# Where the 31-tap convolution of a token mixer starts on VectorE: behind the context's projections instead of behind the filler queue

## The chip, the cores and the metric

The kernel runs on one core of a Trainium2 chip. The metric is the device time of one execution in microseconds. Three executions took 2501.44, 2507.44 and 2507.93 us, median 2507.44. About 0.3% (7.5 us) is what a measurement of this kernel can tell from no change.

## What is computed

The reference is a network of two blocks on 512 tokens of width 1024: 256 tokens of context and 256 latents. The second block has two layers, and each runs four token mixers side by side and multiplies their joined results by `w_out`. In layer 0 both halves go through the mixers; in layer 1 only the latents do, with the context's keys and values.

```
def conformer_conv(a_val, a_gate, conv_w, conv_b, ln_g, ln_b):
    glu = a_val * jax.nn.sigmoid(a_gate)
    y = depthwise_conv(glu, conv_w) + conv_b
    return jax.nn.silu(layer_norm(y, ln_g, ln_b))

def token_mixers(z, k1, k2, v, rope, lam, lam_init, conv_a_w, conv_a_b, ln_a_g, ln_a_b, subln_g,
                 sg_ln_g, sg_ln_b, sg_w, sg_b, conv_d_w, w_out):
    a_val, a_gate, q, _, _, u, sv, bg, cg, xin = z
    y_a = conformer_conv(a_val, a_gate, conv_a_w, conv_a_b, ln_a_g, ln_a_b)
    q1, q2 = qk_heads(q, rope)
    y_b = diff_attention(q1, q2, k1, k2, v, lam, lam_init, subln_g)
    y_c = spatial_gating(u, sv, sg_ln_g, sg_ln_b, sg_w, sg_b)
    y_d = short_conv_mixer(bg, cg, xin, conv_d_w)
    return jnp.concatenate([y_a, y_b, y_c, y_d], axis=-1) @ w_out
```

`z` are the columns of the normalized tokens times one wide matrix. `diff_attention` is softmax attention with two score maps per head, whose weights are subtracted.

## The kernel before, in words

Every fp32 product is three fp32r matmuls (high part by high part, high by low, low by high), L287, L288 and L289 in `mm3`. A weight is loaded by a transfer on SP's queue into a `raw` tile, ScalarE casts the high part (L281, `wh`), and VectorE subtracts it for the low part (L282, `wl`). Results are split for the next product in the same way (L266 on ScalarE, L267 on VectorE).

PSUM has three pools of 512-column tiles: `pm` (4 tiles) for projections and transposes, `px` (3) for scores and small sums, `pa` (1) for the attention's result. In SBUF the tiles named `a` come from one pool of 31 buffers; casts of weights go through three `wh` and three `wl` buffers.

The change is in `_mixers`, which runs once per layer (`l` is 0 or 1). Its parts are closures and generators:

- `gated(f)` makes one half (128 of 256 channels) of the convolution's input: two projections (L1440 and L1441), a zero fill on POOL (L1442), a sigmoid on ScalarE (L1444) and a product on VectorE (L1446), which goes into a padded tile and is appended to `glu`.
- `taps()` is the 31-tap convolution, all of it on VectorE: for each `f` one TENSOR_SCALAR (L1488) and 30 SCALAR_TENSOR_TENSOR (L1490) that add into the tile `ya_f`. It yields every two taps, 15 times per half.
- `qk_of` and `v_of` project queries, keys and values.
- `gating()` is the spatial gating (GELU at L1548 and L1549, its layer norm at L1550 to L1560, product with a second matrix, L1571), `short()` the short convolution, and `conv_norm()` (L1717 to L1736) the layer norm and SiLU (L1733) behind the taps.
- `probs` is one attention item, 128 queries of one head: scores on TensorE (L1647, two `px` tiles), maximum (L1650, L1651), exponential on ScalarE (L1654), reciprocal and factors (L1657, L1658), scaling (L1659, L1660). `mix` transposes its weights (L1238) and multiplies them with the values into `pa`; it runs two items later.
- `fill()` is a queue of filler work for TensorE: in layer 0 the latents' queries, keys and values; then `gated(0)` and `gated(1)`; then the steps of `gating` and `short`; and last the projections by `w_oa`.

The loop at the end runs over the items, 16 in layer 0 (8 of the context with 256 keys, 8 of the latents with 512) and 8 in layer 1. Each turn issues an item's `probs`, one or two steps of the filler, and, once both halves of `glu` exist, some steps of the taps. So the text sets an order of priority; a scheduler then places the instructions of the five engines, and each engine executes its own in that fixed order. An instruction that waits holds up all that stand behind it on the same engine.

Of the kernel before, what the change touches and what calls it, by code (L numbers as in the profile page):

```python
# [1194 lines left out]
def _rotate(K, x, kind, tab):  # L1195

    nc = K.nc
    ps = K.ax_ps()
    nc.tensor.matmul(ps[:, 0:TC], K.perm[kind], x, start=True, stop=True)
    t = K.t2()  # L1200
    nc.vector.tensor_mul(t[:, 0:TC], ps[:, 0:TC], tab[:, 1])
    nc.vector.tensor_mul(x, x, tab[:, 0])
    nc.vector.tensor_add(x, x, t[:, 0:TC])
# [205 lines left out]
def _mixers(K, l, h, z, mod, norm):  # L1409
# [24 lines left out]
    glu = []  # L1434

    def gated(f):

        pv_, pg = K.mm_ps(), K.mm_ps()
        K.proj(W(6 + f), 1, lambda k: h[k], pg[:, a:e], a, e)
        K.proj(W(4 + f), 1, lambda k: h[k], pv_[:, a:e], a, e)  # L1440
        t = K.a4(F32, (P, seqs, TC + 30))  # L1441
        nc.gpsimd.memset(t, 0.0)  # L1442
        s = K.t2()
        nc.scalar.activation(s[:, a:e], pg[:, a:e], AF.Sigmoid)  # L1444
        r = lambda x: x[:, a:e].rearrange("p (s t) -> p s t", s=seqs)
        nc.vector.tensor_mul(t[:, :, 15:15 + TC], r(s), r(pv_))  # L1446
        glu.append(t)

    def qk_of(t, ws, x0, x1):
        ps = K.mm_ps()  # L1450
        K.proj_w([ws], lambda k: h[k], ps[:, x0:x1], x0, x1)
        x = K.t2()
        nc.scalar.copy(x[:, x0:x1], ps[:, x0:x1])
        if x1 == T:
            _rotate(K, x[:, TC:T], 1, tab)
        K.split(t[:, 0, x0:x1], t[:, 1, x0:x1], x[:, x0:x1])
# [3 lines left out]
    def v_of(wv, hv):  # L1460

        vps = K.mm_ps()
        for t in range(2):
            sl = slice(hv[1] + t * P, hv[1] + (t + 1) * P)
            vv = vps[:, t * 256:(t + 1) * 256]
            for kt in range(KD):
                wh, wl = wv[kt // 4]
                K.mm3(vv, h[kt][:, 0, sl], h[kt][:, 1, sl], wh[:, kt % 4, :], wl[:, kt % 4, :],
                      kt == 0, kt == KD - 1)
            v = K.a4(F32R, (P, 2, 4, P))  # L1470
            nc.gpsimd.memset(v.bitcast(F32), 0.0)
            src = vv.rearrange("p (j e d) -> p j e d", j=2, e=2)
            dst = v.rearrange("p x (j e) c -> p x j e c", j=2)
            for g in range(2):
                K.split(dst[:, 0, :, g, 64 * g:64 * g + 64], dst[:, 1, :, g, 64 * g:64 * g + 64], src[:, :, g])
            vz.append(v)
# [4 lines left out]
    def taps():  # L1481
        for f in range(2):
            if f == 0:
                ya_f.append(K.a4())
            y3 = ya_f[0][:, f, a:e].rearrange("p (s t) -> p s t", s=seqs)
            w = lambda i: K.pvc("conv_a_w", (l * 31 + i) * 2 + f)
            x = lambda i: glu[f][:, :, i:i + TC]
            nc.vector.tensor_scalar(y3, x(0), w(0), K.pvc("conv_a_b", l * 2 + f), op0=ALU.mult, op1=ALU.add)  # L1488
            for i in range(1, 31):
                nc.vector.scalar_tensor_tensor(y3, x(i), w(i), y3, op0=ALU.mult, op1=ALU.add)  # L1490
                if i % 2 == 0:
                    yield

    conv = taps()

    def step(gen, n):
        for _ in range(n):
            next(gen, None)
# [12 lines left out]
            qk_of(qp[f], wq[f], 0, TC)  # L1511
    wv = vw(l == 1)
    v_of(wv, HALVES[0])
    if l == 1:
        for f in range(2):
            qk_of(kp[f], wk[f], TC, T)
        for f in range(2):
            qk_of(qp[f], K.weight(W(f)(0)), TC, T)
        v_of(wv, HALVES[1])


    yc = []
# [82 lines left out]
    def fill():  # L1605
        if l == 0:
            for f in range(2):
                qk_of(kp[f], wk[f], TC, T)
                yield
            for f in range(2):  # L1610
                qk_of(qp[f], wq[f], TC, T)
                yield
            v_of(vw(), HALVES[1])
            yield
        for f in range(2):
            gated(f)
            yield
        parts = {"g": gating(), "s": short()}
        for c in "ss" + "g" * nt + "sssgsg":
            next(parts[c])  # L1620
            yield
        y = yc + yd
        for ft in range(KD):
            ps = K.mm_ps()
            K.proj(lambda c: A["w_oa"][l, ft, 0], 1, lambda k: y[k], ps[:, a:e], a, e)
            K.resid(ps, z[ft // 2][:, ft % 2], mod[:, 2], ft, halves)
            yield

    filler = fill()

    yb = []
# [120 lines left out]
    for i, u in enumerate(items):  # L1752
        queue.append((u, probs(*u)))
        step(filler, FS[l][i])
        if len(glu) == 2 and conv is not None:
            step(conv, (3,2)[l])
            if next(conv, 0) == 0:
                conv = None
                tails.append(conv_norm())
        tails = [g_ for g_ in tails if next(g_, 0) is None]  # L1760
        finish(2)
# [141 lines left out]
```

## Time and profile before

| | |
|---|---|
| median of three runs | 2507.44 us |
| the profiled execution | 2502.68 us, of which its span is 2500.9 us |
| TensorE (PE) busy | 2398.7 us, 96% of the span |
| VectorE (DVE) busy | 1618.3 us, 65% |
| ScalarE (ACT) busy | 1106.4 us, 44% |
| mean granted TensorE clock | 0.978 of full speed |
| chain of work that ended last | PE 85%, DVE 6%, DMA 5%, ACT 3% |

Layer 0's mixers take the stretch from about 1552 to 1742 us, layer 1's that from about 2157 to 2300 us. A table by stretch gives, for each engine, its busy time and (in brackets) its number of instructions, then the mean granted clock of TensorE: 1.00 is 2.4 GHz, and a stretch spent at 1.2 GHz counts half. In lists of lines, a mean duration includes the fill of the engine's pipeline, which overlaps the next instruction; the step from one start to the next is a little shorter.

### The profile page before, as it was taken

The numbers are of one execution on the slowest core, as the hardware profiler recorded it, in microseconds if no ns is written. First come the engines' busy times: TensorE is split into PE (matmuls) and PEld (weight loads), VectorE is DVE, ScalarE is ACT, GpSimd is POOL, SyncE is SP. The second block draws the span as 40 slices with busy tenths as digits, with TensorE's granted clock in tenths as the row PEclk, the third lists the DMA queues.
The fourth block names the chain that finished last, engine by engine and source line by source line (L and its number), as shares of the span: only waits on it lengthen the run. The fifth ranks groups of instructions, "written<-read, shape, count | busy, mean of one in ns | idle before, by whom it ended". The sixth has DMA issues, their size and how long they took to land.

```text
span 2500.9 us, 36344 instructions
## 1 busy us (share of the span) xinstructions
PE 2398.7 (96%) x14234; PEld 2066.7 (83%) x14234; DVE 1618.3 (65%) x2953; ACT 1106.4 (44%) x1875; POOL 11.3 (0%) x20
## 2 busy tenths in 40 slices
PE   7999999999998999999999999989999999988998
PEld 4877888788897887778887999867978778977998
DVE  4856445544667675666766676897848564597665
ACT  5643334322544333235546455554523323465543
POOL 0000000000000000000000000000000000000000
PEclk9999999999999999999998999989999999998999
DMA  8565223333323455565347554222336563123553
GB/s 314 192 215 185 85 85 110 127 101 112 110 88 130 150 173 167 200 229 195 117 132 256 181 176 138 79 77 81 124 104 216 171 227 117 64 94 102 187 183 120
DMA packets 113741, 369.71 MB, mean 148 GB/s; under 512 B 12576, under 2 KB 15008, under 8 KB 113568
## 3 DMA queue, kind: packets, MB, share of 16 engines
q1 hardware_dynamic: 113568, 367.38, 44.5%
q8 instruction: 112, 1.84, 0.3%
q14 instruction: 61, 0.50, 0.1%
HBM read 357.89 MB, written 9.44 MB: 147 GB/s over the span
## 4 chain that ended last, share of the span: by engine, by line
PE 85%; DVE 6%; DMA 5%; ACT 3%; issue 1%; SPq 0%; DVEq 0%; ACTq 0%
PE pm L287 23%; PE pm L288 23%; PE pm L289 22%; PE px L287 4%; PE px L289 4%; PE px L288 4%; DMA raw<-in_ada 2%; DVE wl L282 1%; PE pa L423 1%; PE px L313 1%; DVE a L465 1%; PE px L1647 1%; DMA raw<-in_w_inb 1%; DVE a L1490 1%; PE pm L1238 1%
## 5 line engine op out<-in xcount | busy, mean ns | idle before, releaser
L287 PE MATMUL pm<-a,wh 128*128 128x512 f32 (+1 forms) x2432 | 838.3, 346 | 7.4 <-DVE a L267 4.2
L289 PE MATMUL pm<-a,wl 128*128 128x512 f32 (+1 forms) x2432 | 834.0, 344 | 3.6 <-DVE wl L282 3.6
L288 PE MATMUL pm<-a,wh 128*128 128x512 f32 (+1 forms) x2432 | 835.9, 344 | 0.0
L281 ACT CAST wh<-raw 128x1024 fp32r<-128x1024 f32 (+2 forms) x421 | 420.2, 1002 | 810.4 <-PE pm L288 454.2
L282 DVE TENSOR_TENSOR wl<-raw,wh 128x1024 fp32r<-128x1024 f32 (+2 forms) x421 | 487.8, 1161 | 330.3 <-ACT wh L281 326.6
L287 PEld LDWEIGHTS pm<-a,wh 128*128 128x128 f32 x2432 | 462.6, 191 | 78.7 <-ACT wh L281 10.7
L289 PEld LDWEIGHTS pm<-a,wl 128*128 128x128 f32 x2432 | 463.2, 191 | 58.0 <-DVE wl L282 4.6
L288 PEld LDWEIGHTS pm<-a,wh 128*128 128x128 f32 x2432 | 464.1, 191 | 51.7 <-issue 1.0
L287 PE MATMUL pm<-a,a 128*128 128x256 f32 (+2 forms) x844 | 249.8, 302 | 14.8 <-DVE t L368 6.4
L288 PE MATMUL pm<-a,a 128*128 128x256 f32 (+2 forms) x844 | 250.3, 298 | 2.3 <-DVE a L267 1.4
L289 PE MATMUL pm<-a,a 128*128 128x256 f32 (+2 forms) x844 | 247.6, 296 | 0.0
L465 DVE SCALAR_TENSOR_TENSOR a<-raw,cs,a 128x1024 f32<-128x1024 f32 x168 | 211.2, 1279 | 54.0 <-DMA raw<-in_ada 49.8
L287 PEld LDWEIGHTS pm<-a,a 128*128 128x128 f32 x844 | 164.8, 198 | 26.4 <-issue 11.1
L288 PEld LDWEIGHTS pm<-a,a 128*128 128x128 f32 x844 | 166.8, 198 | 6.5 <-DVE a L267 3.2
L289 PEld LDWEIGHTS pm<-a,a 128*128 128x128 f32 x844 | 166.0, 197 | 2.4 <-issue 0.4
L549 DVE SCALAR_TENSOR_TENSOR a<-pm,mod,a 128x256 f32<-128x256 f32 x188 | 87.2, 479 | 82.0 <-PE pm L289 81.0
L287 PE MATMUL pm<-wh,a 128*128 128x512 f32 (+1 forms) x336 | 128.6, 385 | 3.3 <-ACT a L266 3.3
L288 PE MATMUL pm<-wl,a 128*128 128x512 f32 (+1 forms) x336 | 129.9, 387 | 0.0
L289 PE MATMUL pm<-wh,a 128*128 128x512 f32 (+1 forms) x336 | 126.1, 383 | 0.0
L266 ACT CAST a<-t 128x256 fp32r<-128x256 f32 (+2 forms) x173 | 86.0, 503 | 86.2 <-DVE t L1787 37.8
L287 PE MATMUL px<-a,wh 128*128 128x256 f32 (+1 forms) x364 | 120.3, 332 | 0.0
L289 PE MATMUL px<-a,wl 128*128 128x256 f32 (+1 forms) x364 | 119.9, 330 | 0.0
(309 smaller groups left out, 2915.7 us busy)
## 6 DMA issues: line engine op xcount, KB each, us to landing
raw<-in_ada SPq DMA_DIRECT2D x176, 512.0 KB, 4.5
raw<-in_w_m SPq DMA_DIRECT2D x128, 512.0 KB, 4.3
raw<-in_ffn_in SPq DMA_DIRECT2D x88, 512.0 KB, 4.4
raw<-in_w_qk SPq DMA_DIRECT2D x32, 512.0 KB, 3.5
raw<-in_w_v SPq DMA_DIRECT2D x32, 512.0 KB, 3.6
raw<-in_ffn_oa SPq DMA_DIRECT2D x32, 512.0 KB, 3.6
raw<-in_w_inb SPq DMA_DIRECT2D x28, 512.0 KB, 3.6
a<-in_ada SPq DMA_DIRECT2D x16, 512.0 KB, 9.0
```

The costliest lines, as they stand in the source:

```text
L266: self.nc.scalar.copy(hi, src)
L281: nc.scalar.copy(hi, raw)
L282: nc.vector.tensor_sub(lo, raw, hi.bitcast(F32))
L287: mm(out, ah, bh, start=start, stop=False)
L288: mm(out, ah, bl, start=False, stop=False)
L289: mm(out, al, bh, start=False, stop=stop)
L313: self.nc.tensor.matmul(out_ps[:, i * nt + t:i * nt + t + 1], a[:, c0 + t * P:c0 + (t + 1) * P], self.ones[:, 0:1], start=(k == 0), stop=( ...
L423: nc.tensor.matmul(ps[32 * j:32 * j + 32, 0:256], self.cs[:, l // 2, kt, :], raw[:, j, :], start=(kt == 0), stop=(kt == KD - 1), tile_posi ...
L465: nc.vector.scalar_tensor_tensor(s, raw, c, s, op0=ALU.mult, op1=ALU.add)
L549: self.nc.vector.scalar_tensor_tensor(z[:, a:b], ps[:, a:b], gate[:, kt, w:w + 1], z[:, a:b], op0=ALU.mult, op1=ALU.add)
L1238: nc.tensor.transpose(pt[:, s * P:(s + 1) * P], p[:, s * P:(s + 1) * P], K.ident)
L1490: nc.vector.scalar_tensor_tensor(y3, x(i), w(i), y3, op0=ALU.mult, op1=ALU.add)
```

## The change

`gated(0)` and `gated(1)` leave the filler queue and run right behind the context's values, before the first item. The taps get two steps there, and in layer 1 two more behind each of the latents' four query and key projections and behind their values (twelve in all ahead of the loop). In the loop they are stepped in every turn, one step (layer 0) or two (layer 1) and the one of the test for the end, two and three in all, where it was four and three from the turn on in which both halves of `glu` existed. Nothing is computed otherwise.

```
     v_of(wv, HALVES[0])
+    for f in range(2):
+        gated(f)
+    step(conv, 2)
     if l == 1:
         for f in range(2):
             qk_of(kp[f], wk[f], TC, T)
+            step(conv, 2)
         for f in range(2):
             qk_of(qp[f], K.weight(W(f)(0)), TC, T)
+            step(conv, 2)
         v_of(wv, HALVES[1])
+        step(conv, 2)
...
-        for f in range(2):
-            gated(f)
-            yield
         parts = {"g": gating(), "s": short()}
...
         step(filler, FS[l][i])
-        if len(glu) == 2 and conv is not None:
-            step(conv, (3,2)[l])
+        if conv is not None:
+            step(conv, (1, 2)[l])
             if next(conv, 0) == 0:
```

Line numbers of the changed kernel are 6 higher between the first and the last piece, and 3 higher behind it: L1650 there is L1647 here, L1653 is L1650, L1657 is L1654, L1660 is L1657 and L1663 is L1660.

**VectorE, layer 0, the start of the taps.** `a_14451` (before) and `a_14061` (changed) are the accumulators, `sd` an item's statistics, `t` its weights. Before:

```order
L1446 TENSOR_TENSOR a_14346<-t_14348,pm_14284 128x2x256
L1660 SCALAR_TENSOR_TENSOR t_14276<-t_14278,sd_14264,t_14276 128x256
L1488 TENSOR_SCALAR a_14451<-a_14346,pv 128x512
L1490 SCALAR_TENSOR_TENSOR a_14451<-a_14346,pv,a_14451 128x512 x2
L1650 TENSOR_REDUCE sd_14364<-px_14366 128x1
```

Changed:

```order
L1446 TENSOR_TENSOR a_13989<-t_13991,pm_13927 128x2x256
L282 TENSOR_TENSOR wl_14344<-raw_14341,wh_14343 128x1024
L1488 TENSOR_SCALAR a_14061<-a_13989,pv 128x512
L1490 SCALAR_TENSOR_TENSOR a_14061<-a_13989,pv,a_14061 128x512 x4
L282 TENSOR_TENSOR wl_14350<-raw_14347,wh_14349 128x1024
L1490 SCALAR_TENSOR_TENSOR a_14061<-a_13989,pv,a_14061 128x512
L1660 RECIPROCAL sd_14067<-sd_14067 128x2
L1490 SCALAR_TENSOR_TENSOR a_14061<-a_13989,pv,a_14061 128x512
L1661 TENSOR_TENSOR sd_14067<-sd_14067,lt_13697 128x2
L1490 SCALAR_TENSOR_TENSOR a_14061<-a_13989,pv,a_14061 128x512
L1663 SCALAR_TENSOR_TENSOR t_14079<-t_14081,sd_14067,t_14079 128x256
```

The first tap stood behind the sixth item's softmax (row 1684 of the engine's order); it now stands at row 1624, between the first item's maximum and its reciprocal, and all 60 taps stand ahead of the GELU's statistics, up to row 1758.

**VectorE, layer 1, the end of the taps.** Before, the last taps stand behind the eighth and last item's L1660 and behind the layer norm of the gating:

```order
L1560 TENSOR_TENSOR a_19862<-a_19862,a_19854 128x256
L1660 SCALAR_TENSOR_TENSOR t_20198<-t_20200,sd_20186,t_20198 128x512
L1560 TENSOR_TENSOR a_19862<-a_19862,a_19854 128x256
L1490 SCALAR_TENSOR_TENSOR a_19676<-a_19671,pv,a_19676 128x256
L267 TENSOR_TENSOR a_20144<-a_19862,a_20143 128x4x64
L267 TENSOR_TENSOR a_20178<-pm_20179,a_20177 128x4x128
L1490 SCALAR_TENSOR_TENSOR a_19676<-a_19671,pv,a_19676 128x256
```

Changed:

```order
L1660 RECIPROCAL sd_19869<-sd_19869 128x2
L1490 SCALAR_TENSOR_TENSOR a_19423<-a_19418,pv,a_19423 128x256
L1661 TENSOR_TENSOR sd_19869<-sd_19869,lt_19129 128x2
L1490 SCALAR_TENSOR_TENSOR a_19423<-a_19418,pv,a_19423 128x256
L1605 TENSOR_TENSOR t_19714<-t_19714,pm_19970 128x256
L1663 SCALAR_TENSOR_TENSOR t_19881<-t_19883,sd_19869,t_19881 128x512
L1653 TENSOR_REDUCE sd_19950<-px_19952 128x1
L1653 TENSOR_REDUCE sd_20054<-px_20055 128x1
```

The last tap moved from row 2544, behind every item's softmax, to row 2482, ahead of the fourth item's L1660 (L1663 in the changed file) and of the gating's layer norm.

**TensorE, layer 0, behind `conv_norm`.** `px_15189` and `px_15195`, or `px_15333` and `px_15339`, are the broadcast statistics of the convolution's norm; the L1647 (L1650) rows are scores. Before, the scores of the last two items stand there, and other products behind them:

```order
L337 MATMUL px_15189<-first,rs_15181 128x128 x4
L337 MATMUL px_15195<-first,st_15176 128x128 x4
L1647 MATMUL px_15221<-a_13711,a_13713 128x512 x3
L1647 MATMUL px_15222<-a_13711,a_13713 128x512 x3
L1696 MATMUL px_15288<-ind,a_14362 128x2 x2
L1647 MATMUL px_15312<-a_13711,a_13713 128x512 x3
```

Changed:

```order
L337 MATMUL px_15333<-first,rs_15325 128x128 x4
L337 MATMUL px_15339<-first,st_15320 128x128 x4
L1650 MATMUL px_15355<-a_13711,a_13713 128x512 x3
L289 MATMUL pm_15455<-a_14906,wl_15459 128x512
L287 MATMUL pm_15455<-a_15183,wh_15458 128x512
L288 MATMUL pm_15455<-a_15183,wh_15458 128x512
L289 MATMUL pm_15455<-a_15183,wl_15459 128x512
L1650 MATMUL px_15356<-a_13711,a_13713 128x512 x3
L1710 MATMUL px_15416<-first,sq_15417 128x128 x2
L1238 MATMUL pm_15485<-first,t_15366 128x128 x4
```

One item is left behind the norm instead of two, and its transposes (L1238 of `t_15366`) follow its own scores after four product matmuls.

## Rows read from the trace of the kernel before

**Rows 1.** The page: busy time by engine, and the chain that ended last.
```profile
PE 2398.7 (96%) x14234; PEld 2066.7 (83%) x14234; DVE 1618.3 (65%) x2953; ACT 1106.4 (44%) x1875; POOL 11.3 (0%) x20
PE 85%; DVE 6%; DMA 5%; ACT 3%; issue 1%; SPq 0%; DVEq 0%; ACTq 0%
```

**Rows 2.** Busy time by stretch, layer 0: PE, PEld, DVE, ACT, POOL, clock, DMA, GB/s.
```profile
1620.00:1640.00 20.00, 19.33 (x90) 14.88 (x88) 19.30 (x31) 10.60 (x19) 0.00 (x0) 1.00 0.50 170
1640.00:1660.00 20.00, 15.38 (x49) 11.55 (x50) 17.51 (x38) 13.25 (x25) 0.00 (x0) 0.74 0.18 54
1680.00:1700.00 20.00, 16.07 (x86) 13.12 (x86) 18.37 (x40) 10.61 (x25) 0.00 (x0) 0.83 0.05 14
1700.00:1720.00 20.00, 16.33 (x66) 12.23 (x66) 16.06 (x53) 11.79 (x23) 0.00 (x0) 0.74 0.06 15
```

**Rows 3.** The same table, layer 1.
```profile
2220.00:2240.00 20.00, 18.37 (x123) 15.27 (x122) 19.27 (x47) 11.61 (x24) 0.00 (x0) 1.00 0.23 66
2240.00:2260.00 20.00, 8.59 (x47) 6.89 (x45) 20.00 (x69) 9.82 (x22) 0.00 (x0) 0.66 0.10 27
2260.00:2280.00 20.00, 20.00 (x143) 19.65 (x144) 14.50 (x42) 9.98 (x20) 0.00 (x0) 0.83 0.18 54
```

**Rows 4.** Waits of PE in layer 1, and in layer 0: total, times, longest.
```profile
PE px L1707 <- DVE sd L1658: 7.6, 1, 7.6
PE px L313 <- DVE a L1490: 0.6, 1, 0.6
PE px L1647 <- ACT t L1654: 7.3, 3, 4.5
```

**Rows 5.** Busy time ahead of the taps and among them, both layers (columns as above).
```profile
1570.00:1598.00 28.00, 27.91 (x168) 22.90 (x166) 18.17 (x50) 16.33 (x41) 0.00 (x0) 1.00 0.20 67
1598.00:1640.00 42.00, 41.33 (x197) 32.88 (x195) 40.79 (x78) 23.08 (x39) 0.00 (x0) 1.00 0.36 119
2165.00:2193.00 28.00, 28.00 (x215) 25.87 (x213) 14.90 (x34) 11.90 (x26) 0.00 (x0) 1.00 0.19 58
2193.00:2225.00 32.00, 32.00 (x201) 27.21 (x200) 30.57 (x66) 21.32 (x35) 0.00 (x0) 1.00 0.37 123
```

**Rows 6.** DVE by line and shape, layer 0 (1552 to 1742), then layer 1.
```profile
L1490 DVE SCALAR_TENSOR_TENSOR a<-a,pv,a 128x512 f32<-128x512 f32 x60 | 44.1, 739 | 0.1
L1490 DVE SCALAR_TENSOR_TENSOR a<-a,pv,a 128x256 f32<-128x256 f32 x60 | 27.2, 472 | 0.1
```

**Rows 7.** DVE in order of time: start, us, what.
```profile
1666.38 0.67 DVE L1650 TENSOR_REDUCE sd<-px 128x1 f32<-128x512 f32 x1
1666.98 0.73 DVE L1490 SCALAR_TENSOR_TENSOR a<-a,pv,a 128x512 f32<-128x512 f32 x1
1667.64 0.15 DVE L326 SCALAR_TENSOR_TENSOR rs<-rs 128x4 f32<-128x4 f32 x1
...
1668.38 1.21 DVE L282 TENSOR_TENSOR wl<-raw,wh 128x1024 fp32r<-128x1024 f32 x1
1669.52 0.74 DVE L1490 SCALAR_TENSOR_TENSOR a<-a,pv,a 128x512 f32<-128x512 f32 x1
```

**Rows 8.** DVE in order of time, layer 1: five taps in a row, and the last.
```profile
2235.54 2.05 DVE L1490 SCALAR_TENSOR_TENSOR a<-a,pv,a 128x256 f32<-128x256 f32 x5
2237.52 0.15 DVE L1657 RECIPROCAL sd<-sd 128x2 f32<-128x2 f32 x1
...
2259.32 0.47 DVE L1490 SCALAR_TENSOR_TENSOR a<-a,pv,a 128x256 f32<-128x256 f32 x1
```

**Rows 9.** PE in order of time at full clock: 512 columns, 256 columns, scores.
```profile
1613.59 0.40 PE L287 MATMUL pm<-a,wh 128*128 128x512 f32 x1
1613.83 0.39 PE L288 MATMUL pm<-a,wh 128*128 128x512 f32 x1
...
1566.25 0.62 PE L1647 MATMUL px<-a,a 32*128 32x256 f32 x6
1566.81 0.44 PE L1238 MATMUL pm<-first,t 128*128 128x128 f32 x2
...
1567.20 0.28 PE L288 MATMUL pm<-a,a 128*128 128x256 f32 x1
1567.32 0.29 PE L289 MATMUL pm<-a,a 128*128 128x256 f32 x1
```

**Rows 10.** ACT in order of time: behind the convolution's norm in layer 0.
```profile
1708.68 0.62 ACT L266 CAST a<-a 128x512 fp32r<-128x512 f32 x1
1709.20 0.58 ACT L266 CAST a<-pm 128x512 fp32r<-128x512 f32 x1
1709.80 1.28 ACT L1654 ACT_TABLE_LOAD   x1
1711.09 0.69 ACT L1654 ACTIVATE t<-px,sd 128x512 f32<-128x512 f32 x1
```

**Rows 11.** POOL's zero fills in layer 0, and transfers from 1552 to 1612.
```profile
L1442 POOL MEMSET a<- 128x572 f32 x2 | 1.1, 576 | 28.8 <-PE pm L288 28.8
...
raw<-in_w_inb SPq DMA_DIRECT2D x2, 512.0 KB, 3.2
```

## Prediction

> **What bounds the kernel now.** I read the page's busy table first. TensorE is busy for 96% of the span and makes 85% of the chain that ended last [rows 1], so time can come back only where TensorE stands idle or runs at 1.2 GHz. Next I read the tables by stretch around the two mixers, and took as lost, in each 20 us, what is missing from busy time times granted clock. In layer 0 that is 20 - 19.33 = 0.7, 20 - 15.38 x 0.74 = 8.6, 20 - 16.07 x 0.83 = 6.7 and 20 - 16.33 x 0.74 = 7.9, together 23.9 us [rows 2]. In layer 1 it is 20 - 18.37 = 1.6, 20 - 8.59 x 0.66 = 14.3 and 20 - 20 x 0.83 = 3.4, together 19.3 us [rows 3]. In these stretches VectorE is busy for 80% to 100%, and the waits of TensorE name it or an exponential that hangs on it; the largest in layer 1 is one of 7.6 us [rows 4]. Ahead of the taps VectorE has time left: 28 - 18.2 = 9.8 us from 1570 to 1598 and 28 - 14.9 = 13.1 us from 2165 to 2193, and among the taps almost none (40.79 of 42, 30.57 of 32) [rows 5]. So **the taps stand where VectorE is short, behind a stretch in which it is idle**. No more than 23.9 + 19.3 = 43 us can come back.
>
> **Unit prices.** A tap's mean is 739 ns on 512 columns and 472 on 256 [rows 6], with an overlapped part; from start to start a tap takes 1667.64 - 1666.98 = 0.66, a maximum over 512 columns 0.60, the low part of a 1024-column weight 1669.52 - 1668.38 = 1.14, the smallest instruction 0.07 to 0.08 [rows 7]. Five taps on 256 columns take 1.98 us, 0.396 each [rows 8]. TensorE takes 0.24 per product of 512 columns, 0.12 per product of 256, and 0.093 per score product on 256 keys [rows 9]. The sums below are instruction counts of the changed order times these steps.
>
> **Layer 0, ahead of the norm.** TensorE's first product with new values behind the gating's first stretch waits for VectorE's L267 at row 1763. From the first L1446 to that row VectorE has 146 instructions: 60 taps x 0.66 = 39.6, 10 weight parts x 1.14 = 11.4, 12 maxima of 256 at an estimated 0.34 (half of 0.60, and a little) and 2 of 512 = 5.3, and 62 others at some 0.27 on average, estimated from their sizes = 16.7; together 73 us. TensorE's work over the same part is 144 x 0.24 + 160 x 0.12 + 42 x 0.093 + some 2 for transposes = 60 us. Both begin at about the same time, VectorE some 1.6 us later because L1446 waits for the sigmoid. TensorE therefore waits 73 + 1.6 - 60 = 14.6, say **15 us**. The bounds are 11 (some of the 62 priced too high) and 18 (VectorE idles 3% of this part, as it did among the taps). It isn't returned later: behind the taps VectorE has less to do than TensorE. In exchange the losses of 0.7, 8.6 and 6.7 us of 1620 to 1700 go, since the 60 taps that kept VectorE at 97% there stand earlier. Of the first two, part is ScalarE's: GELU and exponential take turns there. That order stays, but three loads of tables fall away, because both sigmoids now stand together. Each took 1.28 us, and the exponential began 1711.09 - 1709.80 = 1.29 behind its start [rows 10], so ScalarE gets 3.9 us. I keep 2 us of loss here, between 0 (the room hides the rest) and 4 (nothing is gained). The Trainium skill, page "ScalarE: Activation LUTs", section "What ACT_TABLE_LOAD costs", puts a switch at about 2.66 us with a drain; no such gap stands between the load and the next exponential in these rows, and by its figure three loads would be 8.0 us, and the 2 us kept would be 0.
>
> **Layer 0, behind the norm.** The last item's transposes now follow its own scores on TensorE. VectorE has 24 instructions from the norm's product to that item's L1660: 11 of 512 columns or the like at 0.60 to 0.66, 4 of 256 at 0.34 to 0.40 and small ones, some 11 us; ScalarE puts two SiLUs, casts and a load of 1.28 us ahead of that item's exponentials, as it did before [rows 10]. With hand-overs the chain is some 13 us, and TensorE's cover 4 products and 6 score products, some 4 us. The loss is **9 us** (7 to 12), where it was 7.9.
>
> Layer 0 together: 15 + 2 + 9 = 26 against 23.9, **2 us worse** (from 6 better, 11 + 0 + 7, to 10 worse, 18 + 4 + 12).
>
> **Layer 1.** The gating's second product waits for VectorE's L267 at row 2528. From the first L1446 VectorE has 60 taps x 0.396 = 23.8, 12 weight parts x 1.14 = 13.7, 14 maxima x 0.60 = 8.4, 6 x 0.66 for L1660 = 4.0, and 22 us of others, estimated by size: 72 us. It starts some 3 us late and, waiting for rotations of the latents' queries and keys, idles perhaps 5: 80 us. TensorE's work up to there is 48 x 0.24 + 340 x 0.12 + 42 score products on 512 keys at some 0.3 + transposes = 68 us. It waits 12 us, and behind it both engines have about equal work (37 and 34 us). The tail of taps in front of the norm, which held TensorE until the last tap at 2259.32 [rows 8] [rows 4], is gone. Loss **12 us** (8 to 17) against 19.3: **7 us better** (2 to 11).
>
> **The rest.** POOL's two zero fills take 0.58 us each and were done 30 us ahead of their use [rows 11]; they now stand just ahead of it, and TensorE's four projections cover them. Without that cover they cost 1.2. The weights of the four projections are asked for earlier on SP's queue, past those of the latents; a transfer lands in 3.2 us [rows 11], and the five raw buffers are filled ahead. I cost that at nothing; without the cover it is one landing, 3.2 us. The twelve early steps in layer 1 add no instruction.
>
> **Sum.** -2 + 7 = 5 us faster: 2502.7 - 5 = 2497.7 for the profiled execution. That execution stands 4.8 us below the median of 2507.4, so I predict 2507.4 - 5 = **2502.5 us**. Its own range is -8 (10 worse, 2 better) to +17 (6 and 11 better): 2490 to 2515.5. About 0.3%, 7.5 us, is what can be told from no change: 5 us is inside it.
>
> **Rivals.**
> - *VectorE's idle time is all that counts.* If TensorE's instructions in layer 0 are placed so that VectorE is only short by what it lacks on the whole, the 9.8 us of idle time come back as a gain in layer 0 and up to 13.1 in layer 1 [rows 5]: together 23, and with the 9-us tail kept a little less, 16 to 23, 2484 to 2491. For it: taps need nothing but `glu`, so they can fill every gap. Against it: the count of layer 0 has VectorE 13 us behind by row 1763, because the taps are placed ahead of its end and not spread over the gap behind it. Chance, with all gains over 7.5 us: 0.37.
> - *Slower: one long wait lowers the clock.* In layer 1, before, the wait of 7.6 us [rows 4] stands in a stretch whose granted clock fell to 0.66, a part of it at 1.2 GHz, and the next stretch still has 0.83 [rows 3]. In layer 0, 0.67 + 4.62 = 5.3 us idle cost 0.7 + 8.6 = 9.3, or 1.75 times as much [rows 2]. If the 15 us come in one or two pieces, they cost 1.75 x 15 = 26, layer 0 loses 26 + 2 + 9 = 37, 13 more than before, and layer 1, where 1.6 + 11.4 = 13 us idle cost 19.3, or 1.5 times as much [rows 3], loses 12 x 1.5 = 18 and gains only 1: 12 slower, 2519.5. It decides if single waits are as long as those two of rows 4. The Trainium skill, page "TensorE: Matmul & The Clock Gate", section "HAM oscillation — how this bites in real kernels", says that idle gaps between bursts drop the array to its lower clock, so that the next burst starts slow; the clocks of 0.66 and 0.83 agree. Against it: a TensorE that waits for VectorE again and again loses little by its own clock, since VectorE sets the pace. Chance, with all losses over 7.5 us: 0.21.
> - *The change does nothing.* The order excludes it: on VectorE the first tap stands 60 rows earlier in layer 0 and 25 in layer 1. Its chance is 0.
>
> **Chances.** My forecast of 5 us lies within the 0.3%: same 0.42, faster 0.37, slower 0.21. Leaving out the ends of both rivals, the range is 2488 to 2518.
>
> **What would show it.** In the changed profile: VectorE at 95% or more in the table by stretch from about 1572 to 1645; TensorE's idle time moved there from 1640 to 1700, some 15 us in short waits for L1653, L1663 or L267 and its L1657; a wait of 6 to 10 us at L1238 behind the norm in layer 0; in layer 1 VectorE over 80% from 2165 on, no wait for the last L1490, and TensorE's loss 12 instead of 19. I am wrong if layer 0's first stretch shows less than 8 us of waits (then it is faster), or if its clock falls below 0.8 in more than one stretch of 20 us (then it is slower).

## The result, and the profile after

The changed kernel is slower: a median of 2528.52 us (2526.30 to 2536.49) against 2504.56 (2501.44 to 2507.93) for the kernel before in the same comparison, a ratio of 1.0101 with a 95% interval of 1.0073 to 1.0129. A second comparison gave 2521.25 against 2507.87, 1.0065 (1.0053 to 1.0077). The profiled execution took 2526.30 us, its span 2524.3. The page of the changed kernel, busy time and chain:

```profile
PE 2410.5 (95%) x14234; PEld 2076.6 (82%) x14234; DVE 1621.8 (64%) x2953; ACT 1101.3 (44%) x1872; POOL 11.6 (0%) x20
PE 84%; DVE 7%; DMA 4%; ACT 3%; issue 2%; SPq 0%; DVEq 0%; ACTq 0%
```

Against [rows 1], TensorE executes the same 14234 instructions and is busy 11.8 us longer; its mean granted clock is 0.974, where it was 0.978. VectorE's share of the chain goes from 6% to 7%. ScalarE has the three instructions fewer that were forecast.

To place the loss I cut the traces of both kernels at three starts: the first score product of layer 0 (1561.72 here, 1552.6 before), the first Relu of its channel mixer (1802.37 here, 1781.51 before), and the first Relu of the part of that channel mixer behind 1950 us. *Layer 0's stretch* is from the first to the second, the *end part* from the third to the last instruction; it holds layer 1. In us, two executions of each kernel:

| | first scores at | layer 0's stretch | end part |
|---|---|---|---|
| before | 1552.6, 1557.4 | 228.9, 229.0 | 535.9, 539.4 |
| changed | 1561.7, 1553.3 | 240.7, 240.4 | 538.5, 538.4 |

So **layer 0 costs 11.6 us, and repeats within 0.3. Layer 1 costs next to nothing**: its end parts lie within the 3.5 us by which those of the kernel before differ. The work ahead of the mixers differs by up to 9 us between executions, in instructions that are the same and stand in the same order. Of the 23.4 us between the two profiled spans of the first comparison 9.1 stand there; in the second pair of profiles none do.

The table by stretch of the changed kernel, layer 0 and then layer 1 (columns as in [rows 2]):

```profile
1580.00:1600.00 20.00, 20.00 (x135) 18.13 (x134) 19.50 (x34) 6.79 (x13) 2.13 (x2) 1.00 0.24 80
1600.00:1620.00 20.00, 15.31 (x87) 13.06 (x86) 20.00 (x46) 6.79 (x24) 0.00 (x0) 0.91 0.00 1
1620.00:1640.00 20.00, 15.42 (x76) 12.26 (x75) 19.59 (x42) 7.82 (x20) 0.00 (x0) 0.83 0.27 92
1640.00:1660.00 20.00, 17.95 (x87) 14.14 (x86) 17.22 (x41) 9.77 (x20) 0.00 (x0) 1.00 0.47 159
1660.00:1680.00 20.00, 18.34 (x82) 13.94 (x81) 12.51 (x29) 16.28 (x29) 0.00 (x0) 0.91 0.17 54
...
1700.00:1720.00 20.00, 19.20 (x99) 14.56 (x99) 17.08 (x39) 11.83 (x27) 0.00 (x0) 1.00 0.10 27
1720.00:1740.00 20.00, 17.59 (x101) 14.71 (x99) 13.18 (x40) 5.63 (x8) 0.00 (x0) 0.91 0.17 45
1740.00:1760.00 20.00, 11.62 (x48) 9.79 (x49) 11.28 (x27) 11.50 (x23) 0.00 (x0) 0.66 0.46 152
...
2180.00:2200.00 20.00, 20.00 (x156) 19.96 (x155) 11.75 (x26) 12.60 (x26) 0.00 (x0) 0.91 0.27 87
...
2240.00:2260.00 20.00, 16.90 (x105) 14.42 (x104) 16.68 (x39) 12.99 (x24) 0.00 (x0) 0.83 0.15 42
2260.00:2280.00 20.00, 13.69 (x79) 12.23 (x79) 15.39 (x54) 11.98 (x28) 0.00 (x0) 0.82 0.13 40
2280.00:2300.00 20.00, 18.81 (x118) 17.14 (x119) 15.27 (x43) 10.91 (x22) 0.00 (x0) 0.76 0.14 41
```

By the measure of the prediction (20 less busy time times clock) layer 0 loses 6.1, 7.2, 2.1 and 3.3 from 1600 to 1680, together 18.7 us **ahead of the norm**, and 0.8, 4.0 and 12.3 from 1700 to 1760, together 17.1 **behind it**: 35.8 against 23.9 in [rows 2], 11.9 more, which is the stretch's growth. In the kernel before, the parts were 0.7 + 8.6 + 6.7 = 16.0 ahead of the norm and 7.9 behind it. So of the 11.9 us 2.7 stand ahead of the norm and 9.2 behind it. Layer 1 loses 1.8 + 6.0 + 8.8 + 5.7 = 22.3 against 19.3 in [rows 3].

What TensorE waited for in these stretches, total, times and longest, first layer 0, then layer 1:

```profile
PE pm L1238 <- DVE t L1663: 16.0, 3, 10.8
PE pm L1238 <- DVE sd L1654: 4.7, 1, 4.7
...
PE pm L287 <- ACT a L266: 7.8, 2, 5.8
PE px L1650 <- ACT t L1657: 3.0, 1, 3.0
```

In layer 0 it is the transposes of an item's weights (L1238) that wait for the end of that item's softmax on VectorE (L1663 is L1660 of the kernel before). TensorE's two rows around the first of these waits, and then VectorE's rows of that time (start, duration, what):

```profile
1601.75 0.62 PE L1650 MATMUL px<-a,a 32*128 32x256 f32 x6
1607.05 0.64 PE L1238 MATMUL pm<-first,t 128*128 128x128 f32 x2 [4.69 <-DVE sd L1654]
...
1601.98 0.15 DVE L1660 RECIPROCAL sd<-sd 128x2 f32<-128x2 f32 x1
1602.06 0.73 DVE L1490 SCALAR_TENSOR_TENSOR a<-a,pv,a 128x512 f32<-128x512 f32 x1
...
1605.77 0.74 DVE L1490 SCALAR_TENSOR_TENSOR a<-a,pv,a 128x512 f32<-128x512 f32 x1
1606.43 0.47 DVE L1663 SCALAR_TENSOR_TENSOR t<-t,sd,t 128x256 f32<-128x256 f32 x1
```

The profile names L1654, the row right behind L1663 on VectorE; the tile that the transposes read is L1663's. From the reciprocal to L1663 are 4.45 us. Four of the rows between are taps, 4 x 0.66 = 2.6 us. The taps' result is first read at 1715.87, by the square at L1725; the weights behind them are needed at once.

The longest wait stands behind the convolution's norm. TensorE, then ScalarE, then VectorE:

```profile
1733.72 0.60 PE L337 MATMUL px<-first,st 128*128 128x128 f32 x4
1748.38 1.12 PE L1238 MATMUL pm<-first,t 128*128 128x128 f32 x4 [10.79 <-DVE t L1663]
...
1736.77 1.28 ACT L1736 ACT_TABLE_LOAD   x1
1738.07 0.81 ACT L1736 ACTIVATE a<-a,pv 128x512 f32<-128x512 f32 x1
1739.44 0.81 ACT L1736 ACTIVATE a<-a,pv 128x512 f32<-128x512 f32 x1
1742.22 1.28 ACT L1657 ACT_TABLE_LOAD   x1
1743.52 0.69 ACT L1657 ACTIVATE t<-px,sd 128x512 f32<-128x512 f32 x1
...
1747.57 0.75 DVE L1663 SCALAR_TENSOR_TENSOR t<-t,sd,t 128x512 f32<-128x512 f32 x1
```

From the broadcast of the norm (L337) over the SiLUs to the last item's weights are 1748.38 - 1733.72 = 14.7 us, and TensorE has 14.7 - 10.8 = 3.9 us of work to put there. The 10.8 us stand in a stretch with a granted clock of 0.66, part of it at 1.2 GHz.

### The profile page after: what moved, and what is told of

Its sections match the earlier page's. It is cut to its first block, busy times and chain, and to the rows that moved or that the text cites. A ratio compares the mean times of both kernels' runs of the same rounds, so it can differ in the third digit from the quotient of the medians.

```text
span 2524.3 us, 36334 instructions
## 1 busy us (share of the span) xinstructions
PE 2410.5 (95%) x14234; PEld 2076.6 (82%) x14234; DVE 1621.8 (64%) x2953; ACT 1101.3 (44%) x1872; POOL 11.6 (0%) x20
## 4 chain that ended last, share of the span: by engine, by line
PE 84%; DVE 7%; DMA 4%; ACT 3%; issue 2%; SPq 0%; DVEq 0%; ACTq 0%
PE pm L287 23%; PE pm L288 22%; PE pm L289 22%; PE px L287 4%; PE px L289 4%; PE px L288 4%; DMA raw<-in_ada 2%; DVE a L1490 1%; PE px L313 1%; PE pa L423 1%; DVE wl L282 1%; DVE a L465 1%; PE pm L1238 1%; PE px L1650 1%; DMA raw<-in_w_up 1%
## 5 line engine op out<-in xcount | busy, mean ns | idle before, releaser
L287 PE MATMUL pm<-a,wh 128*128 128x512 f32 (+1 forms) x2432 | 840.5, 348 | 4.4 <-ACT a L266 2.8
L287 PEld LDWEIGHTS pm<-a,wh 128*128 128x128 f32 x2432 | 464.9, 192 | 73.3 <-ACT wh L281 10.7
L287 PE MATMUL pm<-a,a 128*128 128x256 f32 (+2 forms) x844 | 251.1, 301 | 20.3 <-ACT a L266 10.0
L287 PEld LDWEIGHTS pm<-a,a 128*128 128x128 f32 x844 | 164.8, 197 | 33.3 <-ACT a L266 13.0
L287 PE MATMUL pm<-wh,a 128*128 128x512 f32 (+1 forms) x336 | 129.7, 388 | 5.0 <-ACT a L266 3.3
L266 ACT CAST a<-t 128x256 fp32r<-128x256 f32 (+2 forms) x173 | 86.0, 503 | 92.5 <-DVE t L1790 43.9
L287 PE MATMUL px<-a,wh 128*128 128x256 f32 (+1 forms) x364 | 120.3, 332 | 0.0
```

The source lines that it names most:

```text
L266: self.nc.scalar.copy(hi, src)
L287: mm(out, ah, bh, start=start, stop=False)
```

## The experiments

Three theories stood against each other at the start, under the letters of the expectations. **A:** the early taps fill VectorE's in-order queue in layer 0 and delay the softmax there, and the norm, which now has one item behind it, leaves TensorE uncovered; layer 1 matters little. **B:** the late first scores of the changed kernel's profile belong to the change. **C:** layer 1 is the cause. All edits are against the changed kernel unless it is said otherwise. Medians stand beside the kernel before of the same comparison (2507.79, 2508.48, 2507.87 and 2507.78 us in the four).

### One layer at a time

`l0_only` leaves layer 1 as before; `l1_only` leaves layer 0 as before. The edit of the first:

```
-    for f in range(2):
-        gated(f)
-    step(conv, 2)
+    if l == 0:
+        for f in range(2):
+            gated(f)
+        step(conv, 2)
...
+        if l == 1:
+            for f in range(2):
+                gated(f)
+                yield
...
-            step(conv, (3,2)[l])
+            step(conv, (1, 2)[l])
```

> Only layer 0 has the change; layer 1 is as before. Theory A (layer 0 pays: VectorE's taps ahead of the softmaxes, and the last item behind the convolution's norm): 11 to 14 us slower than before, with the waits of 4.7, 3.5 and 10.8 us at L1238 in layer 0 as in the changed kernel, and layer 1's loss near 19 us as before. Theory B (the 7.6 us by which the changed kernel's profile was late before the first mixer belong to the change, through the order of the transfers): 19 to 22 us slower, and the first scores again some 9 us later than the 1552.6 us of before. Theory C (layer 1 is the cause, layer 0 only looks so): less than 5 us slower.

> Only layer 1 has the change; layer 0 is as before. Theory A: 1 to 5 us slower than before: the tail of taps is gone and the gating's chain (GELU behind three loads of tables, statistics, L267) holds TensorE for some 6 us in its place. Theory C: 15 us slower or more. My prediction as it stood had this one 7 us faster.

Measured: `l0_only` 2526.67 us, ratio 1.0074 (1.0059 to 1.0089), layer 0's stretch 242.6; `l1_only` 2512.25, 1.0015 (1.0003 to 1.0026), stretch 229.0, as before, and end part 539.1. Layer 0 carries the loss, which refutes C; of layer 1 there are at most a few us. By its median `l0_only` stands 18.9 us above the kernel before, more than A's 11 to 14 and near B's 19 to 22. But its first scores came at 1555.3, 2.7 us later and not 9: the time is lost behind them, which refutes B. The two don't add up to the whole, since `l0_only` has an end part of 543.1, 4 to 7 longer than that of the kernel before, although its layer 1 is written as there. Its instructions came out in another order; why that costs so much stays open.

### The place of the taps and of the norm in layer 0

`norm_early` runs three steps of the taps per turn, so that the norm comes some five items earlier. `taps_late` keeps the early projections but starts the taps at the seventh turn, with four steps per turn, as in the kernel before:

```
norm_early:
-            step(conv, (1, 2)[l])
+            step(conv, (2, 2)[l])
taps_late:
-    step(conv, 2)
+    if l == 1:
+        step(conv, 2)
...
-        if conv is not None:
-            step(conv, (1, 2)[l])
+        if (l == 1 or i >= 6) and conv is not None:
+            step(conv, (3, 2)[l])
```

> The change, with one more step of the taps per turn in layer 0 (three in all), so that the convolution's norm is issued some five items earlier; on VectorE all taps stand where they stood. Theory A: the wait of 10.8 us behind the norm in layer 0 goes, 10 to 13 us faster than the changed kernel, and the waits of 4.7 and 3.5 us ahead of it stay. Rival (the end of layer 0 waits for the last item whatever stands before it): within 4 us of the changed kernel, with a wait of 8 us or more for the last L1663.

> The change, but in layer 0 the taps start at the seventh turn, four steps per turn, where they started before; the projections stay early. Theory A, in the form that the taps ahead of the softmaxes make the early waits: no wait over 2 us at L1238 before 1660 us, and 6 to 9 us faster than the changed kernel ahead of the norm. Rival (the early projections make them, by pushing the latents' keys and values back): the early waits stay, within 3 us of the changed kernel there.

Measured: `norm_early` 2509.17 us, 1.0006 (0.9991 to 1.0022), stretch 234.7; `taps_late` 2524.07, 1.0063 (1.0046 to 1.0080), stretch 247.8. TensorE's waits in layer 0, `norm_early`:

```profile
PE pm L1238 <- DVE t L1663: 5.2, 2, 3.5
PE pm L1238 <- DVE sd L1654: 4.7, 1, 4.7
```

And `taps_late`:

```profile
PE pm L1238 <- DVE t L1664: 7.0, 3, 3.2
PE pm L288 <- DVE a L267: 5.7, 1, 5.7
```

With other items behind the norm the wait of 10.8 us is gone, and 240.7 - 234.7 = 6.0 us of the stretch with it, not the 10 to 13 expected. The wait of 4.7 at the first taps stays. In `taps_late` it is the other way round: nothing is lost up to 1620, but the same kinds of wait come later, and this version is slowest of all in layer 0. No wait over 2 us stands at L1238 before 1660, as A had it, but the 6 to 9 us that A expected from that did not come: from 1620 to 1680 it loses 19.1 us, where the changed kernel loses 18.7 from 1600 to 1680.

So the place of the taps is not the whole cause, and the rival in that expectation has a share: the early projections push the items back, wherever the taps stand. VectorE's scalings of an item's weights in the first 40 us behind the first scores, in the kernel before, in `taps_late` and in the changed kernel:

```profile
L1660 DVE SCALAR_TENSOR_TENSOR t<-t,sd,t 128x256 f32<-128x256 f32 x5 | 2.4, 483 | 2.0 <-ACT t L1659 1.9
L1664 DVE SCALAR_TENSOR_TENSOR t<-t,sd,t 128x256 f32<-128x256 f32 x2 | 1.0, 484 | 1.3 <-ACT t L1663 1.3
L1663 DVE SCALAR_TENSOR_TENSOR t<-t,sd,t 128x256 f32<-128x256 f32 x1 | 0.5, 485 | 0.0
```

Five items' softmaxes end there before, two with the projections moved alone, one with the taps moved too. The second item's scores come 14 us behind the first in the kernel before, and 33 in both others. That is why VectorE in `taps_late` is busy for only 9.64, 9.04 and 14.39 us of the three stretches from 1560 to 1620, where the kernel before has 14.19 and 12.99 in the first two: the softmaxes are not there yet, and they come when the taps do.

### Fewer taps, and more cover

`half_taps` leaves out taps 17 to 30 in layer 0 and keeps the norm at its turn. `fs_less` puts 18 filler steps instead of 20 into layer 0's loop, so that two are left as work for TensorE behind it.

```
half_taps:
-            for i in range(1, 31):
+            for i in range(1, 31 if l else 17):
...
-        if conv is not None:
+        if conv is not None and (l or i < 7 or i == 14):
fs_less:
-    FS = ([1] * 8 + [1, 2] * 4, [1] * 4 + [2] * 4)
+    FS = ([1] * 8 + [1, 1, 1, 1, 1, 2, 1, 2], [1] * 4 + [2] * 4)
```

> The change, with taps 17 to 30 of the convolution left out in layer 0 (28 of the 60 instructions, 18.5 us of VectorE); the norm stays at its turn. If the early waits in layer 0 come from taps that stand ahead of the softmaxes on a full VectorE: the waits of 4.7, 3.5 and 1.0 us before 1640 us shrink to under 2 us in all, the wait of 10.8 us behind the norm stays, and the kernel is 6 to 10 us faster than the changed one. If they come from the order of TensorE alone (the latents' rotations that follow one another too closely): the waits stay, under 3 us faster.

> The change, with two filler steps fewer in layer 0's loop (18 instead of 20, as many as the two that gated no longer takes), so that products by w_oa are left for the end. If the wait of 10.8 us behind the norm is there because the filler ran ahead by those two steps: it shrinks to under 5 us, 6 to 10 us faster than the changed kernel. If it is there because only one item is left behind the norm, whatever products follow: it stays over 8 us, within 4 us of the changed kernel.

Measured: `half_taps` 2505.17 us, 0.9986 (0.9971 to 1.0000), stretch 228.0; `fs_less` 2516.60, 1.0037 (1.0024 to 1.0051), stretch 240.2. Waits in layer 0, `half_taps`:

```profile
PE pm L1238 <- DVE t L1663: 8.5, 1, 8.5
PE pm L1238 <- DVE sd L1654: 4.0, 1, 4.0
```

And `fs_less`:

```profile
PE pm L1238 <- DVE t L1663: 12.1, 3, 6.9
```

28 taps of 0.66 are 18.5 us of VectorE; without them the stretch is 240.7 - 228.0 = 12.7 us shorter, though the wait behind the norm is still 8.5 long. From 1600 to 1680 it loses 6.2 us, where the changed kernel loses 18.7. The two later early waits for L1663 (3.5 and 1.7) are gone, but the first, of 4.7, is still 4.0; under 2 us of early waits in all were expected. So the later early waits hang on the load of the taps, and the first one hardly. Whether their place or their load alone makes them is not shown, since no run leaves the same taps out of layer 0 of the kernel before. More cover does shorten the wait behind the norm, by 10.8 - 6.9 = 3.9 us, which lies between the two cases of the expectation, but the stretch stays at 240.2: 20 us by 20 us `fs_less` still loses 7.8 + 10.3 = 18.1 at its tail, with clocks of 0.66 and 0.74, where the changed kernel loses 17.1. So these two steps of cover do not give the time back. Its median is below the changed kernel's, but its profile shows where: its first scores at 1550.6 are the earliest of all profiles, and from there to the end it takes 962.8 us, like the changed kernel (962.6 and 962.1).

### The norm early in layer 0 alone, and layer 1's gating

`l0_norm_early` is `norm_early` in layer 0 with layer 1 as before. `l1_gate_first` is `l1_only` with the gating's first part queued ahead of the short convolution:

```
l1_gate_first:
-        for c in "ss" + "g" * nt + "sssgsg":
+        for c in ("ss" + "g" * nt if l == 0 else "ggss") + "sssgsg":
```

> Layer 0 as in the run with the norm some five items earlier, layer 1 as before. If layer 1's part costs what its run alone showed (4.5 us): 3 to 6 us faster than that run, within 5 us of before on the faster side. If the parts don't add up: slower than before.

> Layer 1 alone changed, with the gating's two stretches ahead of the first two stretches of the short convolution, so that its GELU comes earlier. If the gating's chain (GELU behind loads of tables, statistics, L267) is what holds TensorE where the tail of taps held it: the wait of 5.8 us at L287 for L266 goes, 4 to 9 us faster than the run with layer 1 alone, 0 to 5 us faster than before. Rival (another chain, that of the last items' softmax, takes its place at once): within 3 us of that run.

Measured: `l0_norm_early` 2514.67 us, 1.0027 (1.0014 to 1.0040), stretch 231.4, end part 542.4 (long, as in `l0_only`); `l1_gate_first` 2507.31, 0.9997 (0.9984 to 1.0010), end part 539.5. `l0_norm_early` was expected 3 to 6 us below `norm_early` and stands 5.5 above it: the two layers' parts don't add up. In `l1_gate_first` the gating's wait in layer 1 (L287 for L266) is still 5.3 us long. But the edit did not bring the GELUs forward, as it was meant to: the last one starts 277.1 us behind the start of the end part, where it is 273.4 in `l1_only`. So this run does not tell whether an earlier GELU would help; that its median is 4.9 us lower is not seen in the end part (539.5 and 539.1). The gating's chain in `l1_gate_first`, from the last GELU (L1556) over the layer norm on VectorE to the product:

```profile
2242.40 0.41 ACT L1556 ACTIVATE a<-pm 128x256 f32<-128x256 f32 x1
2242.96 0.75 DVE L1557 BATCH_NORM_STATS2 bs<-a 128x6 f32<-128x256 f32 x2
...
2251.41 0.14 DVE L329 SCALAR_TENSOR_TENSOR rs<-rs 128x2 f32<-128x2 f32 x1
...
2254.03 0.74 ACT L266 CAST a<-a 128x256 fp32r<-128x256 f32 x2
...
2254.83 0.69 PE L287 MATMUL pm<-a,a 128*128 128x128 f32 x2 [5.25 <-ACT a L266]
```

And its ends in the changed kernel:

```profile
2261.04 0.39 ACT L1555 ACTIVATE a<-pm 128x256 f32<-128x256 f32 x1
...
2273.96 0.69 PE L287 MATMUL pm<-a,a 128*128 128x128 f32 x2 [5.84 <-ACT a L266]
```

The chain takes 2254.83 - 2242.40 = 12.4 us and 2273.96 - 2261.04 = 12.9. Its small instructions (0.14 to 0.17 us each in the reciprocal root) stand in VectorE's order between softmax rows and those of the short convolution. The taps were over in both by then; that they still bear on when the chain begins is seen below.

### The noise, and the best of both

`after_again` is the changed kernel and `before_again` the one before, each once more. `norm_early_gate_first` joins the two edits above. `before_norm` is the kernel before with five steps of the taps per turn in layer 0 instead of four:

```
-            step(conv, (3,2)[l])
+            step(conv, (4,2)[l])
```

> The changed kernel once more, nothing edited. In its first profile the first scores of layer 0 came 9.1 us later than before, behind instructions that stand in the same order; in seven other kernels with the same beginning they came between 2 us earlier and 11.8 us later. If that is scatter between executions: the first scores near 1555 us, and a median 14 to 18 us above before, as layer 0 (12) and layer 1 (3) make it. If it belongs to the change: first scores again past 1560 us, and 20 to 24 us slower.

> The kernel before once more, for a second profile. From the first scores to the first hidden product of the channel mixer 228 to 230 us again, whatever the first scores' time; layer 1's wait of 7.6 us ahead of the last taps again.

> The change with the norm some five items earlier in layer 0 and with the gating first in layer 1. If the two remedies add up (17 to 19 us and some 5 us by the medians): 2 to 6 us faster than before. If layer 1's gain of the gating's order was scatter: like the run with the norm early, 0 to 3 us slower than before.

> The kernel before, with five steps of the taps per turn in layer 0 instead of four, so that the norm comes one or two items earlier; the projections stay in the filler. If a norm with more items behind it is worth something by itself: the loss of 7.9 us behind the norm shrinks, 2 to 6 us faster than before. If it was right where it stood: within 3 us of before.

Measured: `after_again` 2521.25 us, 1.0065 (1.0053 to 1.0077); `before_again` 2508.70, 1.0005 (0.9993 to 1.0016), with the wait of 7.6 us in layer 1 at 6.4; their stretches are in the table of the result. `norm_early_gate_first` 2510.68, 1.0021 (1.0009 to 1.0033), stretch 232.0: the two edits don't add up. `before_norm` 2505.04, 0.9990 (0.9979 to 1.0000), stretch 227.5: the best version that computes everything, some 2.8 us below the kernel before, at the edge of what the comparison can tell. Either case of its expectation allows that.

### Why layer 1 gained nothing

The changed kernel's last tap in layer 1 starts at 2251.45, some 29 us earlier than the 2259.32 of [rows 8] when both are counted from the first scores of layer 0 and 11.6 us are taken off for that layer. Yet nothing is won. Theory: several chains on VectorE and ScalarE end within a few us of each other there. Rival: taps still fill VectorE. `l1_half_taps` leaves out taps 17 to 30 in layer 1 of the changed kernel, `before_l1_half` the same of the kernel before, and `l1_short_gate` takes the reciprocal root, the gain and the bias out of the layer norm of layer 1's gating. In the first two, further lines, left out here, keep the norm at its turn:

```
l1_half_taps and before_l1_half:
-            for i in range(1, 31):
+            for i in range(1, 17 if l else 31):
l1_short_gate:
-        r = K.rsqrt(vr, nt)
+        r = K.rsqrt(vr, nt) if l == 0 else vr
...
-            nc.vector.tensor_mul(S[:, t], S[:, t], gw[:, 0])
-            nc.vector.tensor_add(S[:, t], S[:, t], gw[:, 1])
+            if l == 0:
+                nc.vector.tensor_mul(S[:, t], S[:, t], gw[:, 0])
+                nc.vector.tensor_add(S[:, t], S[:, t], gw[:, 1])
```

> The change, with taps 17 to 30 left out in layer 1 (28 of 60 instructions, 11 us of VectorE); the norm stays at its turn. If layer 1's stretch is no longer held by the taps but by the gating's chain: from the channel mixer of layer 0 to the end 536 to 539 us as in the changed kernel (538.4), the wait of TensorE for the gating's L266 stays over 4 us. If the taps still hold it: 4 to 8 us shorter.

> The kernel before, with the same 28 taps left out in layer 1; the norm stays behind the loop. If the taps at the end held TensorE there: the wait of 7.6 us ahead of the last taps goes. If VectorE's load was the whole of it: 5 to 9 us shorter than before from the channel mixer to the end (before: 535.9 and 539.4). If the gating's chain waits right behind: less than 3 us shorter, with a wait for the gating's L266 in place of the other.

> The change, with part of the gating's layer norm left out in layer 1 (the reciprocal root, the gain and the bias: some 7 small and 4 instructions of 256 columns, 2 us of VectorE, but all in one chain). If this chain holds TensorE: its wait for L266 shrinks from 5.8 us to under 2, and the stretch to the end is 3 to 6 us shorter than 538.4. If only VectorE's load counts: 1 to 2 us shorter.

Measured: `l1_half_taps` 2517.03 us, 1.0051 (1.0031 to 1.0072), end part 535.3; `before_l1_half` 2501.26, 0.9971 (0.9954 to 0.9988), end part 530.2; `l1_short_gate` 2520.26, 1.0059 (1.0032 to 1.0086), end part 538.5. Waits of TensorE in layer 1, `l1_half_taps`:

```profile
PE pm L1238 <- DVE t L1663: 5.1, 1, 5.1
PE pm L287 <- ACT a L266: 2.6, 2, 1.9
```

`before_l1_half`:

```profile
PE pm L313 <- DVE ac L574: 2.0, 1, 2.0
PE pm L287 <- ACT a L266: 1.9, 1, 1.9
```

And `l1_short_gate`:

```profile
PE pm L1238 <- DVE t L1664: 4.6, 1, 4.6
PE px L1651 <- ACT t L1658: 3.0, 1, 3.0
PE px L1711 <- ACT t L1658: 2.3, 1, 2.3
```

In the kernel before, the taps do bound layer 1: without half of them its end part is 5.7 to 9.2 us shorter, and no wait is longer than 2.0. In the changed kernel the same cut gives 3.1, less than the 4 to 8 of the one case and more than the nothing of the other. The gating's wait shrinks there from 5.8 to 0.7 (the 1.9 listed for L266 stands behind the mixers, in every one of these kernels), since the last GELU starts 9.1 us earlier (266.1 behind the start of the end part, where it was 275.2); so the taps still bear on when the gating's chain begins. A wait of 5.1 for an item's softmax (L1663) then ends last. Shortening the gating gives nothing at all: its wait of 5.8 is gone, as expected, but the wait for a softmax at L1238 grows from 1.2 to 4.6, and one of 2.3 for an exponential is new; the 3.0 was there. Behind the taps lies the gating, and behind the gating the softmax.

## Why the prediction was wrong

It gave 2502.5 us, 5 below the kernel before; the two comparisons measured 24 and 13.4 above, outside the range. By the traces, from the first scores of layer 0 to the end, the two kernels' executions take 948.3 and 951.8 before and 962.6 and 962.1 after, 10 to 14 us more. The step that failed is the same in both layers: **the sum ends each loss where its wait ends, and puts the clock behind the two longest waits at nothing.** The losses before, 23.9 and 19.3 us, against which it set its own, contain that clock.

Its counts of work can be redone in the changed kernel: from layer 0's first L1446 over the 146 instructions counted; from layer 1's to the end of the wait at the gating's second product; and two stretches behind that.

```profile
1578.70:1653.50 74.80, 65.24 (x362) 54.74 (x360) 73.55 (x148) 29.42 (x69) 2.13 (x2) 0.93 0.23 78
2195.50:2274.00 78.50, 69.09 (x453) 59.84 (x451) 72.37 (x177) 43.71 (x84) 0.95 (x1) 0.95 0.28 88
2274.00:2284.00 10.00, 10.00 (x45) 9.23 (x47) 6.25 (x30) 2.84 (x8) 0.00 (x0) 0.50 0.01 2
2284.00:2300.00 16.00, 14.81 (x101) 13.82 (x102) 12.56 (x29) 9.84 (x20) 0.00 (x0) 0.82 0.18 50
```

- **Layer 0, ahead of the norm: right.** VectorE was counted at 73 us and is busy for 73.55; TensorE's work was put at 60 and is 65.24 x 0.93 = 60.7. 15 + 2 = 17 us of loss were forecast and 18.7 measured. TensorE stands idle for 13.0 us from 1600 to 1680 (80 less its four busy times), at waits for L1663 and L1654 as forecast, and VectorE is full from 1580 to 1640 (19.50, 20.00, 19.59).
- **Layer 0, behind the norm: the mechanism was right, the size wrong.** The step "the loss is 9 us" set a chain of 13 us against 4 us of cover. Measured were 14.7 and 3.9, so 10.8 us idle, and it left out the clock: the stretches lose 16.3 us (17.1 with the 0.8 ahead). The 7 us too few there, some 2 of idle time and 5 of clock, are most of layer 0's error; it forecast 2 worse, and 11.6 were measured. [rows 2] had shown that 5.3 us of idle time cost 9.3; the prediction used that factor for the slower rival alone.
- **Layer 1: right up to the gating's second product, wrong behind it.** VectorE was counted at 72 us and is busy for 72.37; it idles 6.1 where 5 were put; TensorE's work was put at 68 and is 69.09 x 0.95 = 65.6. That loses 12.9 us, and "loss 12 us" was forecast; so far its argument held that VectorE sets the pace and TensorE's clock costs little. Behind the product the prediction put nothing, since "both engines have about equal work". But TensorE came out of its wait of 5.8 us at 1.2 GHz: it is busy for all of the next 10 us at a clock of 0.50, and loses 5.0 there and 16 - 14.81 x 0.82 = 3.9 up to 2300, of which 1.2 are idle time. So layer 1 loses 22.3 us, where it lost 19.3 [rows 3] and 12 were forecast, and 7 us better became about 0 in the trace; `l1_only`, at 4.5 us above (0.8 to 6.5), allows for a little worse. What a remedy would have met next, the three runs above show: taps, gating and softmax stand one behind the other.
- **The rest: right, as far as it can be seen.** No wait for the zero fills or for the four projections' weights stands among the waits of layer 0.
- **The rivals.** "VectorE's idle time is all that counts" is refuted: VectorE's idle time ahead of the taps did fill, and ahead of the norm layer 0 lost 2.7 us more than before. "One long wait lowers the clock" came closest, with 12 us slower. Its total came out close and its working did not: it priced the clock for the early idle time of layer 0, which came as waits of up to 4.7 us and cost 18.7 / 13.0 = 1.4 times as much, not 1.75, and put the wait behind the norm at its bare 9 us, where 17.1 were lost. That the two errors nearly cancel is luck. Its 18 us for layer 1 come nearer to the 22.3 than the 12 of the sum. The Trainium skill, page "TensorE: Matmul & The Clock Gate", section "HAM oscillation — how this bites in real kernels", says that the burst behind an idle gap starts slow; the clock of 0.66 around the 10.8 us wait agrees.
- **What would show it.** The sign for slower, a clock below 0.8 in more than one stretch of layer 0, didn't come: it fell to 0.66 in one alone. Clocks of 0.91, 0.83 and 0.91 ahead of the norm, and 0.76 in layer 1 at which the sign did not look, were enough.

An error of 11.6 - 2 = 9.6 us in layer 0 and one of 7 in layer 1 turn 5 faster into some 12 slower, which is what the traces show from the first scores on. In the profiled execution of the first comparison another 9.1 us lie ahead of the mixers.

## What to carry to other kernels

Work that nothing needs soon is not free in an engine's idle time if its inputs must be made earlier too: here four projections put the second item's scores back by 19 us, the taps then stood among the softmaxes, and the loss ahead of the norm only moved (16.0 us before, 18.7 after). What it leaves behind is worth a look as well: with one item behind the norm 17.1 us were lost there instead of 7.9, and an earlier norm gave 6.0 back. A removed wait is worth only the distance to the next chain, so list what ends second and third, on every engine, before a gain is booked. And set like against like: idle time that a sum forecasts lacks the clock behind it, which a measured loss contains. In these tables the loss was 1.5 to 2.1 times the idle time (23.9 / 12.9 and 19.3 / 13.0 us before, 35.8 / 24.6 and 22.3 / 10.6 after, idle time being 20 less busy time in the same stretches).

## What was not expected of the hardware

The work ahead of the mixers, which no edit here touches, took between 1550.6 us (`fs_less`) and 1564.4 (`half_taps`) up to layer 0's first scores, in 17 profiles, while layer 0's stretch repeated within 0.3 us in both kernels. It is not scatter from one execution to the next alone: the changed kernel's four times of the first comparison (2526.30 to 2536.49 us) all lie above its six of the second (2517.39 to 2525.91). What sets it stays open. In the first 240 us of the changed kernel VectorE waited 28.0 us for weights of `in_ada`, where it was 24.2 before. A difference of a few us between two kernels is better read from the stretch that was edited than from the whole time.
